# Low halves of 28 mixing-stage weight blocks made by VectorE in two steps

## The chip, the cores and the metric

The kernel runs on one core of a Trainium2 chip. The metric is the device time of one execution in microseconds (us); lower is better. The engines in the text are TensorE (PE, with its weight loads as PEld), VectorE (DVE), ScalarE (ACT), GpSimd (POOL) and SyncE (SP), which here only issues DMAs.

## The reference, cut to what matters

The program is a trunk of two layers over 512 tokens of width 1024, in float32:

```
for l in range(DEPTH):                      # DEPTH = 2
    proj = rms_norm(h, attn_norm[l]) @ w_in[l]
    y_a = rwkv7_mixer(proj[..., :896], ...)          # delta-rule recurrence, 4 heads of 64
    y_b = retention_mixer(proj[..., 896:1920], ...)  # 4 heads of 64
    y_c = mla_mixer(proj[..., 1920:], ...)           # latent attention, 8 heads
    h = h + concat(y_a, y_b, y_c) @ w_out[l]
    h = h + swiglu(rms_norm(h, ffn_norm[l]))         # d_ff = 2816
return rms_norm(h, final_norm)
```

Every weight matrix is read once. The sections on the change deal with how a block of weights is prepared for the matrix unit.

## The kernel before

**Numbers in two halves.** PE multiplies in a rounded 32-bit format (F32R). To keep float32 accuracy each operand is split into a high half, the rounded value, and a low half, what the rounding left over. A product is then three matmuls: high weights with high and with low activations, low weights with high activations (`gemm`, whose matmuls are recorded in `mm`, line 253). The product is kept in PSUM tiles, `pd` for these products and `pm` for everything else, four buffers each.

**The stream of weights.** Weights come as 204 blocks, numbered in the order of use, 102 for each layer; most are 128 partitions by 1024 columns (512 KB). `fetch` (line 397) issues a block's DMA on SP's queue into a raw tile `wr` (three buffers; some blocks of the feed-forward part use the single tile `gg`). `convert` then makes `wh`, the high half, with a cast on ACT (line 419), and `wl`, the low half, with a subtraction `wr - wh` (line 420), each in three buffers. The subtraction is done by DVE, except for the blocks listed in `POOL_LO`, where POOL does it, and those in `DMA_LO`, where a DMA with addition does it (lines 415 to 417) and the loop goes on to the next part before line 420. `wnext` keeps about three blocks converted ahead of the matmul that takes them. Blocks 0 to 33 and 102 to 135 are those of the mixing stages: projections, the up-projections of the latents, and the output projection.

**The order of work.** One generator, `dense`, issues the large products; others (`rwkv`, `chain`, `group_norm`, `retnet`, `head`, `attend`) issue the mixers' small work. A driver interleaves them at recording time by a clock and by the delays of table `T`. PE's instructions keep the recorded order; a scheduler places those of the other engines by its own estimates, so a change in one instruction can move its neighbours.

**Names that are used below.**
- `chain` runs the recurrence over 8 chunks for two pairs of heads, b = 0 and 1. Each step makes `R` (DVE, line 864) from PSUM, which PE multiplies; then PE adds into the state sum and DVE makes the next state `Sb` (line 875), which PE multiplies at the next step.
- Lines 806 and 807 are a serial triangular solve on DVE, 31 dependent pairs, up to 149 us in layer 0.
- Lines 1271 to 1274 (DVE) multiply rotary queries by tables; lines 1275 and 1276 (POOL) add and subtract the products into r tiles, which SP writes out to `ro_d` (line 1278) and reads back as rows of the queries (line 1282). Line 1288 (DVE) scales the other query rows out of PSUM.
- Lines 348 to 351 are an inverse square root: two steps on ACT, two on DVE (350, 351). L959 and L960 square a PSUM tile on ACT, L317 makes its low half, L965 and L966 follow.
- L897 and L899 are the end of a group norm (DVE, then POOL with the gate `gg`); L307 and L308 split the result in halves, which the output projection takes. L1319 adds a product to the residual. L992, L994 and L995 are a softmax's maximum, exponential and reciprocal, and L221 scales by it (on DVE or POOL).

Of the kernel before, what the change touches and what calls it, by code (L numbers as in the profile page):

```python
# [11 lines left out]
F32 = mybir.dt.float32  # L12
# [4 lines left out]
ALU = mybir.AluOpType  # L17
# [21 lines left out]
     {'norm1': 0, 'p_rwkv': 3.01, 'p_ret': 3.04, 'p_head': 0, 'p_gn': 2.97, 'p_att': 4.58, 'p_kr': 6.44, 'rwkv1': 3.33, 'rwkv2': 4.39, 'rwkv3': 0, 'rwkv4': 0.0, 'rwkv5': 0.0, 'rwkv6': 3.29, 'rwkv7': 0.0, 'rwkv8': 8.11, 'rwkv9': 1.7, 'rwkv10': 2.94, 'rwkv11': 0.81, 'rwkv12': 4.08, 'rwkv13': 0.02, 'rwkv14': 0.19, 'rwkv15': 0.58, 'rwkv16': 0, 'rwkv17': 0.73, 'rwkv18': 14.15, 'rwkv19': 0, 'rwkv20': 0.42, 'rwkv21': 0.0, 'chain1': 0.23, 'chain2': 0.96, 'chain3': 0.79, 'group_norm1': 2.86, 'group_norm2': 4.88, 'group_norm3': 11.43, 'retnet1': 1.54, 'retnet2': 4.41, 'retnet3': 0, 'retnet4': 1.97, 'retnet5': 0, 'retnet6': 0, 'head1': 8.22, 'head2': 0, 'head3': 8.59, 'head4': 4.4, 'attend1': 0, 'key_rope1': 1.51, 'latent_norm1': 3.79, 'latent_norm2': 4.98, 'latent_norm3': 0.0, 'sums1': 0.75, 'sums2': 7.46, 'sums3': 2.63, 'sums4': 4.1, 'sums5': 3.51, 'sums6': 8.25, 'sums7': 4.8}]  # L39

EN = {'e499': 'd', 'e535': 'd', 'e541': 'd', 'e542': 'd', 'e563': 'd', 'e564': 'd', 'e565': 'p', 'e592': 'd', 'e593': 'd', 'e594': 'd', 'e595': 'd', 'e757': 'd', 'e759': 'p', 'e773': 'p', 'e826': 'd', 'e968': 'p', 'e969': 'd', 'e970': 'd', 'e909': 'd', 'e1037': 'd', 'e1090': 'd', 'e1096': 'p', 'e1097': 'p', 'e1171': 'd', 'e302': 'd', 'e273': 'd', 'c511': 'a', 'c639': 'a', 'c646': 'a', 'c647': 'a', 'c686': 'a', 'c716': 'a', 'c736': 'a', 'c1008': 'a', 'c498': 'd', 'h1': 'p', 'h2': 'd', 'h3': 'p', 'h4': 'd', 'h5': 'd', 'h6': 'd', 's1': 'd', 's2': 'd', 's3': 'd', 's4': 'd', 'z': 'd', 'x0': 'a', 'x1': 'd', 'x2': 'p', 'x3': 'd'}
NU, NR, NW = 29, 8, 3

AHEAD, FETCH = 3, 2
# [148 lines left out]
def tile_trunk(ctx: ExitStack, tc: tile.TileContext, a: dict, out: bass.AP, dbg=None):  # L193
    nc = tc.nc
    act, dve, pool, sp = nc.scalar, nc.vector, nc.gpsimd, nc.sync
# [17 lines left out]
    def E(key):  # L213
        return {"d": Dve, "p": pool, "a": Act}[EN[key]]

    def times(key, o, x, f):

        if EN[key] == "a":
            act.activation(o, x, AF.Identity, scale=f)
        else:  # L220
            {"d": dve, "p": pool}[EN[key]].tensor_scalar(o, x, f, None, ALU.mult)  # L221

    def nm(s):
        uid[0] += 1
        return f"{s}_{uid[0]}"
# [176 lines left out]
    def raw(at=0):  # L402
        while len(stream["raw"]) <= at:
            fetch()
        return stream["raw"].pop(at)

    def convert(at=0):

        t, src, i, j, parts, on = raw(at)
        hi, lo = (wp.tile([P, i * j], F32R, tag=n, name=nm(n)) for n in ("wh", "wl"))  # L410
        for part in range(parts):
            z = slice(part * i * j // parts, (part + 1) * i * j // parts)
            if on in DMA_LO:

                act.activation(lo[:, z], t[:, z], AF.Identity, scale=-1.0)
                pool.dma_start(lo[:, z], src[:, z], accum_op=ALU.add)
                act.copy(hi[:, z], t[:, z])
                continue
            act.copy(hi[:, z], t[:, z])  # L419
            (pool if on in POOL_LO else dve).tensor_tensor(lo[:, z], t[:, z], hi[:, z].bitcast(F32), ALU.subtract)  # L420
        stream["ready"].append((1.0, tuple(z.rearrange("p (i j) -> p i j", i=i) for z in (hi, lo))))

    def load_next(parts=1):
        plan.pop(0)
        fetch(parts)
        convert()
# [14 lines left out]
    def sums(last, down, end, start):  # L441
# [22 lines left out]
        if not start:  # L464
            s4 = add("s4", s2, a12)
            yield operand(s4)
        else:
            yield convert()
# [3 lines left out]
        if down and not start:  # L472
            yield convert()
# [1041 lines left out]
```

## Time and profile before

| | |
|---|---|
| time, median of 3 runs | 1293.65 us (1290.88 to 1296.6) |
| the profiled execution | 1294.58 us, span 1292.8 us |
| mean granted PE clock | 0.993 |
| PE busy | 1264.5 us (98%) |
| DVE busy | 975.8 us (75%) |
| ACT busy | 697.9 us (54%) |
| POOL busy | 107.4 us (8%) |
| line 420 on DVE, blocks from `wr` | 76 instructions, 87.8 us |
| line 420 on POOL | 15 instructions, 32.8 us |

The span runs from the first to the last instruction of one profiled execution; the 1.78 us beside it lie outside all instructions. [...] Blocks 20 to 33 are prepared between about 131 and 291 us, blocks 116 to 129 between about 730 and 845 us.

### The profile page before, as it was taken

What the parts mean: (1) busy time and instruction counts of PE and PEld (TensorE: products, weight loads), DVE (VectorE), ACT (ScalarE), POOL (GpSimd) and SP (SyncE); (2) the same over time, 40 slices, a digit from 0 to 9 for tenths busy, and PEclk for the clock granted to TensorE, in tenths of its full rate; (3) what the DMA queues carried; (4) which work ended last, traced back from release to release, by engine and by line L of the source; (5) the groups of instructions that cost most, each with busy time, mean ns of one, the idle gap of its engine ahead of it and who ended that gap; (6) DMA issues with size and microseconds to landing.
All of it is one profiled execution on the core that took longest, in us unless ns stands there. A gap on an engine that the chain in (4) does not pass through costs nothing.

```text
span 1292.8 us, 20207 instructions
## 1 busy us (share of the span) xinstructions
PE 1264.5 (98%) x7802; PEld 1087.7 (84%) x7802; DVE 975.8 (75%) x1639; ACT 697.9 (54%) x1302; POOL 107.4 (8%) x93
## 2 busy tenths in 40 slices
PE   7999999999999999999999999999999999999997
PEld 5788778678899999999877877876789999999996
DVE  7786995757987777778747696788579877777774
ACT  7834456835554444445566455485555544444454
POOL 1150011111000000000022310121000000000000
PEclk9999999999999999999999999999999999999998
DMA  7435331033233333332532784241122332223231
GB/s 253 137 90 158 97 108 57 26 98 98 82 115 99 98 98 99 108 105 94 180 110 72 173 170 106 72 159 50 50 98 82 113 100 99 98 99 99 83 113 66
DMA packets 69096, 136.12 MB, mean 105 GB/s; under 512 B 29220, under 2 KB 34116, under 8 KB 69000
## 3 DMA queue, kind: packets, MB, share of 16 engines
q1 hardware_dynamic: 66040, 128.23, 32.0%
q0 software_dynamic: 1728, 5.51, 2.2%
q8 instruction: 61, 1.00, 0.3%
q10 hardware_dynamic: 1232, 1.09, 0.2%
q14 instruction: 35, 0.29, 0.1%
HBM read 122.48 MB, written 9.18 MB: 102 GB/s over the span
## 4 chain that ended last, share of the span: by engine, by line
PE 87%; DVE 7%; ACT 3%; DMA 2%; issue 1%; POOL 0%; SPq 0%; DVEq 0%; ACTq 0%; POOLq 0%
PE pd L253 60%; PE pm L253 25%; PE pm L260 2%; DMA wr<-in_wts_dram 1%; DMA u<-in_xT_dram 1%; DVE wl L420 1%; DVE u L1288 1%; DVE r L806 0%; DVE r L350 0%; DVE r L317 0%; DVE r L1477 0%; DVE u L308 0%; DVE u L1255 0%; DMA PC<-in_prm_dram 0%; DVE r L807 0%
## 5 line engine op out<-in xcount | busy, mean ns | idle before, releaser
L253 PE MATMUL pd<-u,wh 128*128 128x256 f32 (+1 forms) x3136 | 759.9, 335 | 9.5 <-ACT wh L419 6.2
L253 PEld LDWEIGHTS pd<-u,wh 128*128 128x128 f32 x3136 | 530.4, 191 | 72.7 <-issue 7.4
L253 PE MATMUL pd<-u,wl 128*128 128x256 f32 (+1 forms) x1568 | 519.3, 331 | 1.2 <-DVE wl L438 1.0
L253 PEld LDWEIGHTS pd<-u,wl 128*128 128x128 f32 x1568 | 299.4, 191 | 30.3 <-DVE wl L438 1.5
L253 PE MATMUL pm<-u,wh 128*128 128x512 f32 (+1 forms) x800 | 211.8, 352 | 0.0
L253 PEld LDWEIGHTS pm<-u,wh 128*128 128x128 f32 x800 | 139.0, 190 | 17.9
L419 ACT CAST wh<-wr 128x1024 fp32r<-128x1024 f32 (+3 forms) x91 | 88.6, 979 | 116.3 <-issue 58.3
L437 ACT CAST wh<-r 128x512 fp32r<-128x512 f32 x144 | 87.4, 618 | 102.4 <-PE pm L253 51.4
L253 PE MATMUL pm<-u,wl 128*128 128x512 f32 (+1 forms) x400 | 140.3, 351 | 0.0
L420 DVE TENSOR_TENSOR wl<-wr,wh 128x1024 fp32r<-128x1024 f32 (+3 forms) x76 | 87.8, 1158 | 31.1 <-ACT wh L419 30.9
L437 ACT CAST wh<-wr 128x512 fp32r<-128x512 f32 x108 | 67.0, 620 | 79.3 <-PE pm L253 53.8
L438 DVE TENSOR_TENSOR wl<-r,wh 128x512 fp32r<-128x512 f32 x144 | 97.5, 687 | 8.0 <-ACT wh L437 6.0
L438 DVE TENSOR_TENSOR wl<-wr,wh 128x512 fp32r<-128x512 f32 x108 | 74.2, 689 | 24.4 <-ACT wh L437 22.3
L253 PEld LDWEIGHTS pm<-u,wl 128*128 128x128 f32 x400 | 75.7, 189 | 10.3
L1400 DVE TENSOR_TENSOR u<-u,pm 128x512 f32<-128x512 f32 x64 | 43.7, 684 | 43.3 <-PE pm L253 43.3
L420 POOL TENSOR_TENSOR wl<-wr,wh 128x1024 fp32r<-128x1024 f32 (+3 forms) x15 | 32.8, 2193 | 510.6 <-ACT wh L419 510.6
L253 PE MATMUL pm<-u,u 32*32 32x32 f32 (+4 forms) x728 | 66.9, 277 | 0.7 <-DVE u L758 0.2
L253 PEld LDWEIGHTS pm<-u,u 32*32 32x32 f32 (+3 forms) x728 | 50.3, 156 | 18.4 <-issue 10.5
L419 ACT CAST wh<-gg 128x1024 fp32r<-128x1024 f32 x32 | 33.6, 1050 | 42.3 <-issue 27.7
L448 DVE TENSOR_TENSOR r<-r,wr 128x512 f32<-128x512 f32 x72 | 49.5, 687 | 0.6
L420 DVE TENSOR_TENSOR wl<-gg,wh 128x1024 fp32r<-128x1024 f32 x32 | 39.1, 1222 | 7.8 <-ACT wh L419 7.8
L253 PE MATMUL pd<-u,u 96*128 96x512 f32 (+3 forms) x128 | 41.8, 442 | 0.9 <-ACT u L994 0.9
(276 smaller groups left out, 1611.5 us busy)
## 6 DMA issues: line engine op xcount, KB each, us to landing
wr<-in_wts_dram SPq DMA_DIRECT2D x142, 512.0 KB, 3.5
gg<-in_wts_dram SPq DMA_DIRECT2D x32, 512.0 KB, 3.4
wr<-in_wts_dram SPq DMA_DIRECT2D x22, 384.0 KB, 3.0
u<-in_xT_dram SPq DMA_DIRECT2D x7, 512.0 KB, 5.2
wl<-in_wts_dram POOLq DMA_DIRECT2D x5, 512.0 KB, 7.8
tb<-tab_d SPq DMA_DIRECT2D x8, 256.0 KB, 4.5
r<-r SPq DMA_DIRECT2D x32, 64.0 KB, 2.0
h_d<-u SPq DMA_DIRECT2D x4, 512.0 KB, 2.9
```

The lines of the kernel that those rows point to most:

```text
L253: tc.keep_in_program_order(nc.tensor.matmul(o, lhsT, rhs, start=start, stop=stop, skip_group_check=True))
L260: tc.keep_in_program_order(nc.tensor.transpose(o, x, idn))
L419: act.copy(hi[:, z], t[:, z])
L420: (pool if on in POOL_LO else dve).tensor_tensor(lo[:, z], t[:, z], hi[:, z].bitcast(F32), ALU.subtract)
L437: act.copy(hi[:, z], t)
L438: dve.tensor_tensor(lo[:, z], t, hi[:, z].bitcast(F32), ALU.subtract)
L448: E(key).tensor_tensor(o, x, y, ALU.add)
L1288: dve.tensor_tensor(q_[0:64, par, :], ps[rows], fq[rows], ALU.mult)
L1400: dve.tensor_tensor(hk(m), hk(m), ps, ALU.add)
```

## The change

For the 28 blocks of a new tuple `HALVES`, the low half is made by DVE in two subtractions of half the columns each (512 and 512; 384 and 384 for blocks of 768), whatever `POOL_LO` says. The new lines stand behind the branch for `DMA_LO`, which is as before.

```diff
+HALVES = (20, 21, 22, 23, 24, 25, 26, 27, 28, 29, 30, 31, 32, 33, 116, 117, 118, 119, 120, 121, 122, 123, 124, 125, 126, 127, 128, 129)
 ...
             if on in DMA_LO:
 ...
                 continue
             act.copy(hi[:, z], t[:, z])
+            if on in HALVES:
+                for z in (slice(0, i * j // 2), slice(i * j // 2, i * j)):
+                    dve.tensor_tensor(lo[:, z], t[:, z], hi[:, z].bitcast(F32), ALU.subtract)
+                continue
             (pool if on in POOL_LO else dve).tensor_tensor(lo[:, z], t[:, z], hi[:, z].bitcast(F32), ALU.subtract)
```

With `DMA_LO = (113, 114, 115, 118, 119, 120, 121, 122, 124, 125, 126)` and blocks 25, 30, 120, 122 and 127 of the 28 in `POOL_LO`. In the changed kernel the lines from 41 on have moved down by 2 and those behind the new branch by 6; the new subtraction is line 424, and L1288 of before is L1294. PE's order is the same in both kernels. What moves on the other engines:

On DVE in layer 0, from the last two rotary products (L1273, L1274) on. `wl_1836` is block 26. Before:

```order
L1273 TENSOR_TENSOR r_328_1740<-pd_1657,tb_1733 128x512
L1274 TENSOR_TENSOR r_327_1739<-pd_1657,tb_1732 128x512
L1288 TENSOR_TENSOR u_1750<-pd_1759,fB_1592 64x512 x2
L875 SCALAR_TENSOR_TENSOR Sb_317_1721<-pm_1723,dsc_598,EX 128x128
L875 SCALAR_TENSOR_TENSOR Sb_321_1727<-pm_1729,dsc_598,EX 128x128
L420 TENSOR_TENSOR wl_1836<-wr_1833,wh_1835 128x1024
L350 SCALAR_TENSOR_TENSOR r_340_1791<-r_340_1791,r_338_1788 128x512
L864 TENSOR_TENSOR R_342_1814<-pm_1815,EX 128x128
```

The same place in the changed kernel, where `wl_1761` is block 25 and L881, L870, L352 and L353 are L875, L864, L350 and L351 of before:

```order
L1279 TENSOR_TENSOR r_328_1745<-pd_1662,tb_1738 128x512
L1280 TENSOR_TENSOR r_327_1744<-pd_1662,tb_1737 128x512
L424 TENSOR_TENSOR wl_1761<-wr_1758,wh_1760 128x512 x2
L1294 TENSOR_TENSOR u_1755<-pd_1765,fB_1596 64x512 x2
L352 SCALAR_TENSOR_TENSOR r_340_1797<-r_340_1797,r_338_1794 128x512
L881 SCALAR_TENSOR_TENSOR Sb_317_1726<-pm_1728,dsc_598,EX 128x128
L353 SCALAR_TENSOR_TENSOR r_339_1796<-r_340_1797,r_339_1796 128x512
L881 SCALAR_TENSOR_TENSOR Sb_321_1732<-pm_1734,dsc_598,EX 128x128
L972 TENSOR_TENSOR r_338_1794<-pm_1707,r_339_1796 128x512
L870 TENSOR_TENSOR R_342_1820<-pm_1821,EX 128x128
```

Block 25's two halves, which POOL made in one step before, stand ahead of L1288 and Sb; L350 has moved ahead of the first Sb; block 26 has moved behind both R.

On DVE in layer 1, at the same lines. Before:

```order
L1273 TENSOR_TENSOR r_1536_8283<-pd_8237,tb_8276 128x512
L1274 TENSOR_TENSOR r_1535_8282<-pd_8237,tb_8275 128x512
L875 SCALAR_TENSOR_TENSOR Sb_1474_7970<-pm_8255,dsc_7013,EX 128x128
L875 SCALAR_TENSOR_TENSOR Sb_1478_7976<-pm_8262,dsc_7013,EX 128x128
L864 TENSOR_TENSOR R_1543_8319<-pm_8320,EX 128x128
```

In the changed kernel, with block 127 as `wl_8316`:

```order
L1279 TENSOR_TENSOR r_1536_8300<-pd_8254,tb_8293 128x512
L1280 TENSOR_TENSOR r_1535_8299<-pd_8254,tb_8292 128x512
L424 TENSOR_TENSOR wl_8316<-wr_8313,wh_8315 128x512 x2
L881 SCALAR_TENSOR_TENSOR Sb_1474_7987<-pm_8272,dsc_7027,EX 128x128
L881 SCALAR_TENSOR_TENSOR Sb_1478_7993<-pm_8279,dsc_7027,EX 128x128
L870 TENSOR_TENSOR R_1543_8337<-pm_8338,EX 128x128
```

Two halves now stand between the rotary products and the two Sb. On POOL at this place, where block 127 stood between the two rotary sums. Before:

```order
L416 DMA wl_8195<-in_wts_dram 128x768
L1275 TENSOR_TENSOR r_1534_8281<-r_1534_8281,r_1536_8283 128x512
L420 TENSOR_TENSOR wl_8299<-wr_8296,wh_8298 128x1024
L1276 TENSOR_TENSOR r_1535_8282<-r_1535_8282,r_1537_8284 128x512
L221 TENSOR_SCALAR u_8442<-u_8442,rs_8459 128x384
```

In the changed kernel:

```order
L418 DMA wl_8212<-in_wts_dram 128x768
L1281 TENSOR_TENSOR r_1534_8298<-r_1534_8298,r_1536_8300 128x512
L1282 TENSOR_TENSOR r_1535_8299<-r_1535_8299,r_1537_8301 128x512
L223 TENSOR_SCALAR u_8462<-u_8462,rs_8479 128x384
L223 TENSOR_SCALAR u_8498<-u_8498,rs_8515 128x384
```

The second rotary sum follows the first at once. A third place is block 29 in layer 0 on DVE. Before:

```order
L221 TENSOR_SCALAR u_2562<-u_2562,rs_2569 128x512
L420 TENSOR_TENSOR wl_2595<-wr_2592,wh_2594 128x1024
L897 TENSOR_TENSOR r_544_2542<-r_544_2542,u_524 128x512
L995 RECIPROCAL rs_2611<-ssum_2610 128x2
L1319 TENSOR_TENSOR u_2369<-u_2369,pd_2644 128x512
L221 TENSOR_SCALAR r_550_2563<-r_550_2563,rs_2611 128x256
```

In the changed kernel:

```order
L223 TENSOR_SCALAR u_2571<-u_2571,rs_2578 128x512
L424 TENSOR_TENSOR wl_2604<-wr_2601,wh_2603 128x512
L903 TENSOR_TENSOR r_544_2551<-r_544_2551,u_524 128x512
L424 TENSOR_TENSOR wl_2604<-wr_2601,wh_2603 128x512
L1001 RECIPROCAL rs_2621<-ssum_2620 128x2
L1325 TENSOR_TENSOR u_2377<-u_2377,pd_2654 128x512
```

L897 (now L903) goes between the two halves.

## The prediction

> **What bounds the kernel now.** I read the page first, then the busy time of the two stretches in which the changed blocks are made, then the instructions of TensorE (PE) there that had to wait, then what VectorE (DVE) and GpSimd (POOL) did ahead of those waits. From the page, the engines and the two groups of the operation that the change touches:
>
> ```profile
> PE 1264.5 (98%) x7802; PEld 1087.7 (84%) x7802; DVE 975.8 (75%) x1639; ACT 697.9 (54%) x1302; POOL 107.4 (8%) x93
> L420 DVE TENSOR_TENSOR wl<-wr,wh 128x1024 fp32r<-128x1024 f32 (+3 forms) x76 | 87.8, 1158 | 31.1 <-ACT wh L419 30.9
> L420 POOL TENSOR_TENSOR wl<-wr,wh 128x1024 fp32r<-128x1024 f32 (+3 forms) x15 | 32.8, 2193 | 510.6 <-ACT wh L419 510.6
> ```
>
> PE is busy for 98% of the span. A change that touches only DVE and POOL matters where PE waits for them. The changed blocks lie in about 125 to 275 us (layer 0) and 750 to 920 us (layer 1); a row is start and length, then busy time of PE, its weight loads, DVE, ACT and POOL, the granted clock and the DMAs:
>
> ```profile
> 125.00:275.00 150.00, 145.64 (x958) 113.07 (x957) 116.96 (x256) 90.24 (x210) 20.11 (x14) 1.00 0.28 79
> 750.00:920.00 170.00, 164.76 (x1039) 128.47 (x1038) 121.04 (x267) 96.67 (x218) 24.93 (x20) 0.99 0.37 98
> ```
>
> PE's idle time is 4.36 us in the first and 5.24 us in the second. All of it together is 9.6 us, 0.74% of the span: no gain can be larger. The clock is full, so nothing is to be had there. In layer 0 these PE instructions waited where a changed block is near (start, duration, instruction, idle time before it and what ended it):
>
> ```profile
> 172.39 0.49 PE L253 MATMUL pm<-R,u 128*128 128x128 f32 x2 [0.85 <-DVE R L864]
> 177.66 0.49 PE L253 MATMUL pm<-Sb,u 128*128 128x128 f32 x2 [0.44 <-DVE Sb L875]
> 178.76 0.49 PE L253 MATMUL pm<-u,u 128*128 128x128 f32 x2 [0.16 <-ACT u L877]
> 185.67 0.49 PE L253 MATMUL pm<-Sb,u 128*128 128x128 f32 x2 [0.46 <-DVE Sb L875]
> ```
>
> All four belong to the recurrence over chunks: R and Sb are small DVE operations, and what counts is what stands in front of them on DVE. No matmul of these stretches waits for a low half (wl), so a first half that is ready earlier buys nothing.
>
> **What is really changed.** Of the 28 blocks, 118 to 122 and 124 to 126 are in DMA_LO and leave the loop before the new lines: 20 blocks change. 17 of them go from one DVE step to two. Three (25, 30, 127) go from one POOL step to two DVE steps.
>
> **Splitting (17 blocks).** On DVE the next instruction starts before the last one's end, so starts are what to count:
>
> ```profile
> 131.34 1.22 DVE L420 TENSOR_TENSOR wl<-wr,wh 128x1024 fp32r<-128x1024 f32 x1
> 132.47 0.38 DVE L807 TENSOR_TENSOR r<-r,r 128x224 f32<-128x224 f32 x1
> 163.06 0.68 DVE L967 TENSOR_TENSOR r<-r,u 128x512 f32<-128x512 f32 x1
> 163.66 0.68 DVE L1231 TENSOR_TENSOR r<-r,rB 128x512 f32<-128x512 f32 x1
> ```
>
> 1024 columns hold DVE for 1.13 us, 512 for 0.60. Two halves cost 1.20, that is 0.07 more; 17 blocks make 1.2 us. DVE has 33 and 49 us of idle time in the two stretches, which hides it; it counts only where a block stands directly ahead of something PE waits for (one place, below). In the serial triangle solve up to 149 us the extra pieces also fill slots between dependent steps, so I take nothing there. SyncE's queue changes in three places: the ro_d writes go ahead of a weight load twice, and a weight load goes behind the gg load. Those weight loads run up to three blocks ahead of their use, and the products of the blocks in between cover them: nothing. Without that cover such a load would cost its wait for gg.
>
> **Block 25 (layer 0).** Rows of DVE, ACT and POOL around it:
>
> ```profile
> 167.88 2.13 DVE L350 SCALAR_TENSOR_TENSOR r<-r,r 128x512 f32<-128x512 f32 x1
> 172.05 0.28 DVE L864 TENSOR_TENSOR R<-pm,EX 128x128 f32<-128x128 f32 x1
> 175.84 1.38 DVE L1288 TENSOR_TENSOR u<-pd,fB 64x512 f32<-64x512 f32 x2
> 177.26 0.61 DVE L875 SCALAR_TENSOR_TENSOR Sb<-pm,dsc,EX 128x128 f32<-128x128 f32 x2
> 179.03 0.69 DVE L350 SCALAR_TENSOR_TENSOR r<-r,r 128x512 f32<-128x512 f32 x1
> 169.68 0.59 ACT L960 ACTIVATE r<-pm 128x512 fp32r<-128x512 f32 x1
> 167.05 2.41 POOL L420 TENSOR_TENSOR wl<-wr,wh 128x1024 fp32r<-128x1024 f32 x1 [69.69 <-ACT wh L419]
> 175.50 1.28 POOL L1275 TENSOR_TENSOR r<-r,r 128x512 f32<-128x512 f32 x1 [6.04 <-PE pm L253]
> 176.75 1.27 POOL L1276 TENSOR_TENSOR r<-r,r 128x512 f32<-128x512 f32 x1
> ```
>
> The gain: the same L350 takes 0.69 us at 179.03 and 2.13 at 167.88, while POOL makes block 25; it ends at 170.01, 0.55 after POOL. With POOL's step gone, this 1.44 goes. R then starts at about 170.95 instead of 172.05, since the L317 ahead of it (0.60) still needs ACT's L960, which ends at 170.27. That clears PE's 0.85 wait.
>
> The loss: the two halves now stand between L1274 and L1288, and L350 (0.60) moves ahead of Sb. From R to L1288 it was 3.79, so the first half is due at 174.75. L1275, which was at 175.50, comes 1.1 earlier as well: 174.4 to 175.7. The half has two inputs in SBUF as L350 had, so I let it wait and end 0.55 after POOL, at 176.25. Who goes next is told by the only place where two DVE steps met two POOL steps:
>
> ```profile
> 707.13 2.04 DVE L728 TENSOR_TENSOR u<-u,r 64x512 f32<-64x512 f32 x2 [0.57 <-ACT r L719]
> 706.63 1.29 POOL L1162 TENSOR_TENSOR u<-r,tb 128x512 f32<-128x512 f32 x1 [2.83 <-DVE r L1159]
> 707.88 0.66 POOL L733 TENSOR_TENSOR dsc<-r,emid 128x7 f32<-128x7 f32 x1
> ```
>
> They took turns: the second L728 ends at 709.17, 0.63 after L733. So here L1276 (1.27) goes next, and the second half ends near 177.95. Then L1288 twice (1.2) and L350 (0.6): Sb starts at 179.7, 2.45 later than before. PE's rows at 178.76 and 185.67 had 0.16 and 0.46 of waiting, which this lateness eats. Net +1.8 us. Bounds: with no collision the halves end at 175.95, L350 is held by its ACT input until about 177.5 (an estimate: the row at 179.03 less the wait gained), Sb starts at 178.1, net +0.2; with one POOL step waited for, Sb at 178.65, net +0.8.
>
> **Block 127 (layer 1).** The halves again stand right behind L1274, directly ahead of Sb:
>
> ```profile
> 828.52 0.68 DVE L1274 TENSOR_TENSOR r<-pd,tb 128x512 f32<-128x512 f32 x1
> 829.34 0.80 DVE L875 SCALAR_TENSOR_TENSOR Sb<-pm,dsc,EX 128x128 f32<-128x128 f32 x2
> 828.75 1.27 POOL L1275 TENSOR_TENSOR r<-r,r 128x512 f32<-128x512 f32 x1 [8.60 <-DVE r L1273]
> 830.00 2.35 POOL L420 TENSOR_TENSOR wl<-wr,wh 128x1024 fp32r<-128x1024 f32 x1
> 830.43 0.39 PE L253 MATMUL pm<-Sb,u 128*128 128x128 f32 x2
> 843.40 1.22 DVE L420 TENSOR_TENSOR wl<-wr,wh 128x1024 fp32r<-128x1024 f32 x1
> 846.21 1.12 PE L253 MATMUL pd<-u,u 96*128 96x512 f32 x2 [0.86 <-ACT u L994]
> ```
>
> POOL's 2.35 goes, and L1276 moves up behind L1275, onto the halves. The first is due at 829.12, waits for L1275 until 830.02 and ends at 830.57; L1276 runs to 831.8; the second ends at 832.35. Sb starts at 832.3 instead of 829.34, 2.9 late. PE took it 0.40 after its start at 177.66, so at 830.43 there was 0.7 of slack. Net +2.2; +0.3 with no collision, +1.1 with one POOL step. PE has no wait between there and 846.21, so this lateness arrives whole. At 843.40 block 129 holds up the score row maximum behind PE's 0.86 wait: its split adds 0.07, call it 0.1.
>
> **Blocks 29 and 30 (layer 0).** Block 30's halves stand among the residual additions, where POOL is done; cover is DVE's idle time between them. Block 29's halves let L897 in between:
>
> ```profile
> 256.06 1.53 DVE L420 TENSOR_TENSOR wl<-wr,wh 128x1024 fp32r<-128x1024 f32 x1
> 257.51 0.68 DVE L897 TENSOR_TENSOR r<-r,u 128x512 f32<-128x512 f32 x1
> 258.32 1.29 POOL L899 TENSOR_TENSOR r<-r,gg 128x512 f32<-128x512 f32 x1 [1.15 <-PE pd L253]
> 261.04 0.19 PEld L253 LDWEIGHTS pd<-u,wh 128*128 128x128 f32 x1 [0.54 <-DVE u L308]
> ```
>
> L897, POOL's L899, a cast and L308 lead to PE's weight load. L897 can start up to 0.6 earlier, against a wait of 0.54; as block 29 runs stretched beside POOL (1.53 against 1.22) I take -0.4, between 0 and -0.54.
>
> **How sharing is priced.** One pair says that not every POOL operation holds DVE up:
>
> ```profile
> 228.02 0.69 DVE L317 TENSOR_TENSOR r<-u,r 128x512 fp32r<-128x512 f32 x1 [0.68 <-ACT r L314]
> 227.29 1.24 POOL L221 TENSOR_SCALAR u<-u,rs 128x384 f32<-128x384 f32 x1 [5.21 <-DVE rs L995]
> ```
>
> L317 keeps its 0.69 beside a TENSOR_SCALAR; L350 did not beside a TENSOR_TENSOR. L1275 and L1276 are TENSOR_TENSOR, so I price them like L350. [...]
>
> **The sum.** +1.8 + 2.2 + 0.1 - 0.4 = +3.7 us. The profiled execution took 1294.58, of which 1292.8 is the span; it would become 1298.3 with a span of 1296.5. The median of the three runs, 1293.65, is 0.93 below that execution, so the forecast is 1297.3, say 1297.
>
> **Rivals.**
> [...]
> 2. One turn only: both halves run once the first POOL step is over. +0.8 + 1.1 + 0.1 - 0.4 = +1.6: 1295.3.
> 3. Faster, by the relief of DVE at 167.88: if L350's ACT input is early enough for Sb to start before 177.3, the waits 0.85, 0.44, 0.46 and 0.54 all go, 2.3 us, and layer 1 stays: 1291.4. Against it: 1.2 us of halves stand ahead of Sb.
> 4. Clearly slower: R and Sb stay late at each chunk step, so that PE pays for all of DVE's added time: 1.2 for the splits, 3.6 for three blocks, four POOL steps of 1.28, less 1.44: +8.5, 1302. It decides once Sb in both layers starts over 4 us late. Against it: PE's slack between steps.
>
> **Numbers.** Forecast 45%, rival 1 22%, rival 2 18%, rival 3 8%, rival 4 7%. The range takes in rivals 1 and 2 and a bit of what single runs differ by (1290.88 to 1296.6): 1291.5 to 1299.5. A measurement here tells about 0.5%, 6.5 us, from no change. Faster than 1287.2 would need two thirds of all of PE's idle time: 2%. Slower than 1300.1 is rival 4 and the forecast's edge: 8%. Within: 90%.
>
> **What would show it.** In the changed profile L350 in front of the second R should take 0.69; POOL should have 12 of these steps; the first half of block 25 and of block 127 should be stretched to over 1.2 us, with Sb and PE's matmul on it late by 2 us or more. [...] It is wrong altogether if the granted clock moves, or if PE's idle time grows at places with no changed block.

## The result, and the profile after

The changed kernel takes 1298.91 us (median; 1296.67 to 1302.29) where the kernel before takes 1293.74 us: a ratio of 1.0038, with a 95% interval of 1.0025 to 1.0051. That is 5.2 us slower (3.2 to 6.6 by the interval). The profiled execution took 1302.29 us with a span of 1300.5 us; it is the longest of these runs, so its span is read beside two later profiles of the same kernel.

The page of the changed kernel, the engines and the POOL group of the low halves:

```profile
PE 1266.2 (97%) x7802; PEld 1089.7 (84%) x7802; DVE 982.1 (76%) x1662; ACT 697.7 (54%) x1302; POOL 101.6 (8%) x90
L426 POOL TENSOR_TENSOR wl<-wr,wh 128x1024 fp32r<-128x1024 f32 (+3 forms) x12 | 25.7, 2148 | 441.8 <-ACT wh L421 441.8
```

POOL has 12 of these steps instead of 15. DVE is busy 6.3 us longer and PE 1.7 us, while the span is 7.7 us longer: 6.0 us of the added time is PE waiting. Of these, 2.25 us lie before 125 us (idle time 8.08 us before, 10.33 now), where no changed block is made; the two later profiles of the changed kernel have 8.47 and 8.45 us there, so most of the 2.25 belongs to this one execution. The two stretches again, in the columns used ahead of the result:

```profile
125.00:275.00 150.00, 143.27 (x935) 112.96 (x934) 119.84 (x270) 89.64 (x209) 16.17 (x12) 0.98 0.27 76
750.00:920.00 170.00, 163.51 (x1026) 128.50 (x1026) 127.83 (x282) 99.56 (x221) 24.93 (x22) 0.99 0.41 105
```

PE's idle time grew from 4.36 to 6.73 us and from 5.24 to 6.49; in the second stretch the changed kernel runs 5 to 8 us behind, and with the two last waits of the old stretch, which now lie at 926.6 and 927.3, it is 7.40. So 2.4 and 2.2 us were added, 4.5 us in all; the two later profiles give 4.5 and 4.6. The clock of the first stretch, 1.00 before, is 0.98. The PE instructions that carry this:

```profile
180.66 0.80 PE L255 MATMUL pm<-Sb,u 128*128 128x128 f32 x2 [4.27 <-DVE Sb L881]
190.33 0.49 PE L255 MATMUL pm<-Sb,u 128*128 128x128 f32 x2 [0.15 <-DVE Sb L881]
838.13 0.49 PE L255 MATMUL pm<-Sb,u 128*128 128x128 f32 x2 [1.96 <-DVE Sb L881]
854.13 1.13 PE L255 MATMUL pd<-u,u 96*128 96x512 f32 x2 [0.99 <-ACT u L1000]
```

The waits of 0.85 (R), 0.44, 0.16 and 0.46 us in layer 0 are now one of 4.27 and one of 0.15, both at Sb. In layer 1 there was no wait at Sb; now there is one of 1.96. What DVE and POOL did ahead of the first (the second row is the R that PE had waited for, the third the first half of block 25 alone, the fourth both halves):

```profile
167.77 0.69 DVE L352 SCALAR_TENSOR_TENSOR r<-r,r 128x512 f32<-128x512 f32 x1
171.23 0.28 DVE L870 TENSOR_TENSOR R<-pm,EX 128x128 f32<-128x128 f32 x1
175.03 1.49 DVE L424 TENSOR_TENSOR wl<-wr,wh 128x512 fp32r<-128x512 f32 x1
175.03 3.17 DVE L424 TENSOR_TENSOR wl<-wr,wh 128x512 fp32r<-128x512 f32 x2
178.12 1.38 DVE L1294 TENSOR_TENSOR u<-pd,fB 64x512 f32<-64x512 f32 x2
180.25 0.35 DVE L881 SCALAR_TENSOR_TENSOR Sb<-pm,dsc,EX 128x128 f32<-128x128 f32 x1
174.68 1.29 POOL L1281 TENSOR_TENSOR r<-r,r 128x512 f32<-128x512 f32 x1 [76.99 <-PE pm L255]
175.92 1.72 POOL L1282 TENSOR_TENSOR r<-r,r 128x512 f32<-128x512 f32 x1
```

The first half started at 175.03, waited for POOL's first rotary sum (end 175.97) and ended at 176.52, 0.55 us behind it. Then POOL's second sum had its turn (end 177.64), and the second half ended 0.56 us behind that, at 178.20. At the 0.60 us from start to start that 512 columns took in the kernel before (163.06 to 163.66), they would have held DVE for 1.20 us; they held it for 3.09. Layer 1 is the same once more (both halves in one row; the first alone took 1.46 us):

```profile
834.69 3.12 DVE L424 TENSOR_TENSOR wl<-wr,wh 128x512 fp32r<-128x512 f32 x2
837.74 0.60 DVE L881 SCALAR_TENSOR_TENSOR Sb<-pm,dsc,EX 128x128 f32<-128x128 f32 x2
834.33 1.27 POOL L1281 TENSOR_TENSOR r<-r,r 128x512 f32<-128x512 f32 x1 [8.61 <-DVE r L1279]
835.57 1.70 POOL L1282 TENSOR_TENSOR r<-r,r 128x512 f32<-128x512 f32 x1
```

One thing stands in this profile that no term of the sum had, though the forecast had named it as a sign that it is wrong: the granted clock (the third column from the right) falls around the end of the 4.27 us wait and stays low behind it.

```profile
175.00:180.00 5.00, 1.39 (x10) 1.06 (x8) 4.96 (x6) 2.52 (x4) 2.65 (x2) 0.90 0.41 120
180.00:185.00 5.00, 4.34 (x17) 4.15 (x18) 3.85 (x10) 0.82 (x4) 0.00 (x0) 0.50 0.69 194
185.00:190.00 5.00, 5.00 (x26) 4.24 (x25) 3.99 (x7) 1.29 (x4) 0.00 (x0) 0.92 0.04 9
```

Three theories were put to the test. Theory 1: the halves collide with POOL's rotary sums and make Sb late. Theory 2: it is DVE's added work as such (splits, three blocks more) that costs. Theory 3, added later: a long wait of PE also costs clock.

### The profile page after: what moved, and what is told of

It is laid out like the page before. It is cut to its first block, busy times and chain, and to the rows that moved or that the text cites. A ratio compares the mean times of both kernels' runs of the same rounds, so it can differ in the third digit from the quotient of the medians.

```text
span 1300.5 us, 20233 instructions
## 1 busy us (share of the span) xinstructions
PE 1266.2 (97%) x7802; PEld 1089.7 (84%) x7802; DVE 982.1 (76%) x1662; ACT 697.7 (54%) x1302; POOL 101.6 (8%) x90
## 3 DMA queue, kind: packets, MB, share of 16 engines
q10 hardware_dynamic: 1232, 1.09, 0.2%
## 4 chain that ended last, share of the span: by engine, by line
PE 90%; DVE 5%; ACT 3%; DMA 1%; issue 1%; SPq 0%; DVEq 0%; ACTq 0%
PE pd L255 61%; PE pm L255 27%; PE pm L262 2%; DMA wr<-in_wts_dram 1%; DVE wl L424 1%; DVE r L812 0%; DMA u<-in_xT_dram 0%; DVE r L1483 0%; DVE u L1294 0%; DVE r L319 0%; DVE r L813 0%; ACT u L1000 0%; DVE r L744 0%; DVE wl L426 0%; ACT u L309 0%
## 5 line engine op out<-in xcount | busy, mean ns | idle before, releaser
L426 DVE TENSOR_TENSOR wl<-wr,wh 128x1024 fp32r<-128x1024 f32 (+3 forms) x59 | 67.5, 1148 | 27.5 <-ACT wh L421 27.2
L426 POOL TENSOR_TENSOR wl<-wr,wh 128x1024 fp32r<-128x1024 f32 (+3 forms) x12 | 25.7, 2148 | 441.8 <-ACT wh L421 441.8
```

## The experiments

**Which blocks carry the loss.** First the blocks 25 and 127 alone, then the 17 splits alone.

```diff
-HALVES = (20, 21, 22, ..., 33, 116, ..., 129)
+HALVES = (25, 127)
```

> Only blocks 25 and 127 are made in halves by VectorE; the 17 splits and block 30 are as before. In layer 1 the order at the place is that of the changed kernel, in layer 0 only the second half of block 25 stands behind the rotary products, the first stands four microseconds ahead of them. Theory 1 (collision: a half that stands beside the rotary sums waits for GpSimd): layer 1 as in the changed kernel, a wait of PE of 2.0 us at Sb; in layer 0 one half stretched to about 1.4 us instead of two, Sb 1.75 us earlier than in the changed kernel, the wait there about 2.5 us instead of 4.27. Sum against before about +2.8 us, 1296.5. Theory 2 (the 17 splits carry the loss): within 1 us of before.

Measured: 1296.30 us against 1292.48, ratio 1.0031 (1.0019 to 1.0043), by the ratio 4.0 us slower. The half of block 25 that is left behind the rotary products, and PE's two waits at Sb:

```profile
175.09 1.49 DVE L424 TENSOR_TENSOR wl<-wr,wh 128x512 fp32r<-128x512 f32 x1
178.32 0.49 PE L255 MATMUL pm<-Sb,u 128*128 128x128 f32 x2 [1.83 <-DVE Sb L881]
836.69 0.49 PE L255 MATMUL pm<-Sb,u 128*128 128x128 f32 x2 [1.96 <-DVE Sb L881]
```

Layer 1 is as in the changed kernel. In layer 0 the one half took 1.49 us again and the wait was 1.83, less than the 2.5 expected. The waits alone add only 1.9 us to those of before (1.83 and 1.96 in the place of 0.85, 0.44, 0.16 and 0.46); the time is 1.2 us above the expected sum, and in this profile the clock is at 0.68 between 180 and 185 us, which is taken up below.

```diff
-HALVES = (20, 21, 22, ..., 33, 116, ..., 129)
+HALVES = (20, 21, 22, 23, 24, 26, 27, 28, 29, 31, 32, 33, 116, 117, 123, 128, 129)
```

> Only the 17 blocks that VectorE made already are made in halves; 25, 30 and 127 stay with GpSimd in one step. Theory 1 (collision at the rotary sums): no wait of PE over 1 us at either Sb, the time within 1 us of before (0.07 us for each block, 1.2 us, hidden). Theory 2 (the splits carry the loss): 3 to 5 us slower than before.

Measured: 1291.91 us against 1292.48, ratio 0.9999 (0.9988 to 1.0010). The waits in layer 0 are nearly those of before again:

```profile
172.25 0.49 PE L255 MATMUL pm<-R,u 128*128 128x128 f32 x2 [0.85 <-DVE R L870]
177.53 0.49 PE L255 MATMUL pm<-Sb,u 128*128 128x128 f32 x2 [0.43 <-DVE Sb L881]
185.76 0.49 PE L255 MATMUL pm<-Sb,u 128*128 128x128 f32 x2 [0.69 <-DVE Sb L881]
```

So the 17 splits cost nothing that can be measured; theory 2 in this form falls. The loss is in the blocks that moved. The split of block 129 can be seen where it was expected: PE's wait behind it is 0.99 us here and 0.87 in the run with blocks 25 and 127 alone, where block 129 is whole.

**One step instead of two.** Blocks 25 and 127 go to DVE in one step each.

```diff
-HALVES = (20, 21, 22, ..., 33, 116, ..., 129)
+HALVES = ()
-POOL_LO = (0, 8, 12, 13, 25, 30, 35, ..., 122, 127, 130, 137, 140)
+POOL_LO = (0, 8, 12, 13, 30, 35, ..., 122, 130, 137, 140)
```

> Blocks 25 and 127 go to VectorE, but each in one step of 1024 columns; nothing is split, block 30 stays with GpSimd. In the order, block 25 then stands ahead of the rotary products, block 127 right behind them as in the changed kernel. Theory 1 (collision, the two engines taking turns step by step): one step meets one wait. In layer 1 it waits for the first rotary sum alone, ends about 1.1 us after it, and PE's wait at Sb is about 0.9 us instead of 1.96; in layer 0 there is no collision, no wait over 1 us at Sb. Sum against before +0.5 us, 1294.2. Theory 2 (it is VectorE's added work that counts, not the steps): the same lateness in layer 1 as in the changed kernel, 2 us.

Measured: 1294.30 us against 1292.48, ratio 1.0010 (0.9996 to 1.0024). Layer 1:

```profile
832.10 1.99 DVE L426 TENSOR_TENSOR wl<-wr,wh 128x1024 fp32r<-128x1024 f32 x1
834.01 0.60 DVE L881 SCALAR_TENSOR_TENSOR Sb<-pm,dsc,EX 128x128 f32<-128x128 f32 x2
831.73 1.27 POOL L1281 TENSOR_TENSOR r<-r,r 128x512 f32<-128x512 f32 x1 [8.61 <-DVE r L1279]
832.98 2.23 POOL L1282 TENSOR_TENSOR r<-r,r 128x512 f32<-128x512 f32 x1
834.41 0.49 PE L255 MATMUL pm<-Sb,u 128*128 128x128 f32 x2 [0.82 <-DVE Sb L881]
```

The whole block ends at 834.09, 1.09 us behind the first sum, and it is now POOL's second sum that stands still, 2.23 us for work of 1.27. PE's wait is 0.82 us, 0.9 expected. The same columns, cut in two, cost PE 1.96. The number of steps decided here: the one step waited once, the two halves twice.

**The collision taken away.** The changed kernel, with the two rotary sums on DVE.

```diff
-EN = {..., 'e1096': 'p', 'e1097': 'p', ...}
+EN = {..., 'e1096': 'd', 'e1097': 'd', ...}
```

> The changed kernel, with the two rotary sums on VectorE too, so that GpSimd runs nothing beside the halves; VectorE has two more steps ahead of Sb in each layer. Theory 1 (collision): each half takes 0.69 us and holds VectorE for 0.60, the four steps hold it for 2.4 us where the two halves held it for 3.1; Sb is 0.7 us earlier in both layers, PE's waits fall to about 3.6 and 1.3 us, and the time is 1.4 us below the changed kernel's: 1297.5, and lower if the half clock behind the long wait goes too. Theory 2 (no collision, only VectorE's own time ahead of Sb counts): 1.2 us later in each layer, 2.4 us above the changed kernel: 1301.3.

Measured:

```profile
174.69 0.69 DVE L1281 TENSOR_TENSOR r<-r,r 128x512 f32<-128x512 f32 x1
175.89 1.29 DVE L424 TENSOR_TENSOR wl<-wr,wh 128x512 fp32r<-128x512 f32 x2
831.06 1.29 DVE L424 TENSOR_TENSOR wl<-wr,wh 128x512 fp32r<-128x512 f32 x2
179.64 0.49 PE L255 MATMUL pm<-Sb,u 128*128 128x128 f32 x2 [3.56 <-DVE Sb L881]
832.66 0.49 PE L255 MATMUL pm<-Sb,u 128*128 128x128 f32 x2 [1.32 <-DVE Sb L881]
```

Two halves take 1.29 us instead of 3.17, DVE does four steps in less time than it needed for two, and the waits are 3.56 and 1.32 us, 3.6 and 1.3 expected. This shows the collision: DVE has more to do and PE waits less. The time does not follow: 1298.99 us, ratio 1.0050 (1.0035 to 1.0065), where 1297.5 was expected for 0.7 us less waiting in each layer. The mean granted clock of these five runs was 0.990 to 0.994, which leads to theory 3; what is left at equal clock stands at the end of this section.

**Is it the waiting that costs clock?** The changed kernel again, and the changed kernel with TensorE kept busy in the long wait. The extra matmuls write to the tile that the next product clears.

```diff
+            if (l, b, n) == (0, 0, 1):
+                for _ in range(16):
+                    tc.keep_in_program_order(nc.tensor.matmul(ps, blk, EX, start=True, stop=True, skip_group_check=True))
             mm(pR, GL(b, n).rearrange("p w t -> p (w t)"), uv, True, n == 0)
```

> The changed kernel once more, beside before on the same chip, for a second profile. Theory 1 (collision): PE's waits at Sb are 4.3 us in layer 0 and 2.0 us in layer 1 again, 4.5 us more of waiting than in before. Theory 3 (a long wait of PE also costs clock): behind the 4.3 us wait the granted clock is at one half for 3.4 to 6.8 us, as in the first profile, which costs 1.7 to 3.4 us more, in every run; the time 5 to 7 us above before, mean clock lower by 0.001 or more. If the low clock stood there by chance in the first profile, it does not come back at this place.

> The changed kernel with 16 extra matmuls of 512 columns that TensorE runs while it waits for Sb in layer 0; nobody uses their result, and the tile is overwritten by the next product. They fill about 3.7 of the 4.3 us, so Sb comes at the same time as in the changed kernel. Theory 3 (it is the idle TensorE that brings the half clock): no half clock behind 180 us, and the time 1.7 to 2.4 us below the changed kernel run beside it. If the low clock comes from anything else (chance, the load of the chip): a low clock there as often as without the extra matmuls, and no difference in time.

Measured beside the same runs of before (1293.91 us): the changed kernel 1301.31 us, ratio 1.0052 (1.0033 to 1.0072); with the extra matmuls 1297.04 us, ratio 1.0026 (1.0010 to 1.0041), which is more than the 1.7 to 2.4 us of gain expected. First the changed kernel, PE's wait and then the busy times and clock of the 5 us around its end:

```profile
181.54 0.49 PE L255 MATMUL pm<-Sb,u 128*128 128x128 f32 x2 [4.28 <-DVE Sb L881]
```

```profile
180.00:185.00 5.00, 3.46 (x17) 3.27 (x18) 4.47 (x10) 0.83 (x4) 0.00 (x0) 0.74 0.74 213
```

The same two views of the kernel with extra matmuls:

```profile
177.26 3.79 PE L866 MATMUL pm<-EX 128*128 128x512 f32 x16
181.94 0.49 PE L255 MATMUL pm<-Sb,u 128*128 128x128 f32 x2 [0.66 <-DVE Sb L884]
```

```profile
180.00:185.00 5.00, 4.03 (x25) 3.19 (x24) 4.89 (x12) 1.21 (x5) 0.00 (x0) 1.00 0.88 226
```

Sb comes equally late in both (181.13 and 181.53, against 156.10 and 156.48 for the same matmul at the start of the stretch). With PE busy the clock stood at 1.00 there. A second pair, with 7 extra matmuls in front of the late Sb of layer 1 as well:

```diff
+            if (l, b, n) in ((0, 0, 1), (1, 0, 7)):
+                for _ in range(7 if l else 16):
```

> The changed kernel a third time, as the partner of the next run and for one more profile. Theory 1: PE's waits 4.3 and 2.0 us. Theory 3: half clock behind the first wait for 3.4 or 6.8 us once more; 5 to 7 us above before.

> The changed kernel with TensorE kept busy in both waits: 16 extra matmuls in layer 0 as before, and 7 in front of the late Sb of layer 1 (1.6 of its 2.0 us). Theory 3: no low clock behind 180 us nor behind the Sb of layer 1; 2 to 4 us below the changed kernel beside it, and the same lateness of Sb, so that 4 to 5 us above before remain at the same clock. If the low clock comes by chance: no difference from the changed kernel.

Measured beside 1292.87 us for before: the changed kernel 1298.31 us, ratio 1.0048 (1.0032 to 1.0064), a wait of 4.25 us and the clock at 0.66 between 180 and 185 us; both waits filled 1297.74 us, ratio 1.0039 (1.0027 to 1.0052), the clock at 1.00 in both places. Expected were 2 to 4 us below the changed kernel; this pair gives 0.6 us, which alone cannot be told from nothing. All 23 runs of the changed kernel have a mean of 1299.4 us, all 17 with filled waits 1297.4: 2.0 us less, plus or minus 1.3 (twice the standard error). The mean clock was 0.993 and 0.995.

Set side by side, PE's longest wait near 178 to 182 us and the clock behind it:

| kernel | wait, us | lowest clock of a 5 us window, 175 to 190 us |
|---|---|---|
| changed, three profiles | 4.27, 4.28, 4.25 | 0.50, 0.74, 0.66 |
| sums on DVE | 3.56 | 0.66 |
| blocks 25 and 127 alone | 1.83 | 0.68 |
| block 25 by DMA, three profiles (below) | 1.02, 1.02, 1.02 | 1.00, 1.00, 1.00 |
| both kernels with the wait filled | 0.66, 0.62 | 1.00, 1.00 |
| before, splits, whole steps | 0.44, 0.43, 0.34 | 1.00, 1.00, 1.00 |

**The gain alone.** The kernel before with block 25's low half made by an adding DMA, and then the 12 splits of layer 0 with it.

```diff
-DMA_LO = (113, 114, ...)
+DMA_LO = (25, 113, 114, ...)
```

> The kernel before with one change: the low half of block 25 is made by an adding DMA, as it is for blocks 118 to 122, so that neither GpSimd nor VectorE makes it; nothing is split. Theory 1 (collision): L350 in front of the second R takes 0.69 us instead of 2.13, PE's wait of 0.85 us at R goes and the waits of 0.44, 0.16 and 0.46 behind it shrink; 0.9 to 1.9 us faster than before, 1291.2, if nothing else moves. Theory 2 (VectorE's total work sets the end): 1 us at most, no change at these waits.

> As the last one, and with 12 blocks of layer 0 (20 to 24, 26 to 29, 31 to 33) made by VectorE in halves. Theory 1: the splits are hidden, within 0.7 us of the last one. Theory 2: each split costs, 0.8 us or more slower than the last one.

> The kernel before with block 25's low half by an adding DMA, once more, since the first comparison ended at the edge of what can be told (0.999, 0.998 to 1.000). Theory 1: Sb 0.7 us earlier as in the first profile, 0.7 to 1 us faster than before. If that was chance: ratio 1.000.

Measured: ratio 0.9990 (0.9979 to 1.0000) the first time and 0.9998 (0.9988 to 1.0009) the second; with the splits 0.9990 (0.9975 to 1.0004). Rows of the first:

```profile
168.44 0.68 DVE L352 SCALAR_TENSOR_TENSOR r<-r,r 128x512 f32<-128x512 f32 x1
170.97 0.28 DVE L870 TENSOR_TENSOR R<-pm,EX 128x128 f32<-128x128 f32 x1
171.53 0.69 DVE L319 TENSOR_TENSOR r<-r,r 128x512 fp32r<-128x512 f32 x1 [0.27 <-ACT r L966]
177.55 0.49 PE L255 MATMUL pm<-Sb,u 128*128 128x128 f32 x2 [1.02 <-DVE Sb L881]
```

L350's stretch and PE's wait at R are gone, as expected, but the next wait, at Sb, grows from 0.44 to 1.02 us, and the one after it from 0.46 to 0.83, where both were expected to shrink: DVE now idles for ACT (0.27 us) and Sb comes only 0.7 us earlier. PE reaches the Sb matmul of the next step 29.97 us after the one that waited at 155.58, where it took 30.67 before; the second profile has 29.99. A gain of that size lies at the edge of what the plain times tell.

**At equal clock.** Each run on record has its mean granted clock, so the kernels can also be compared at the same clock. This is a reading of the runs above and not one more experiment, and it takes the cost of a lower clock out, also where a wait brings it. A straight line in the clock is fitted, with one offset for each kernel and one for each of the three sets of runs. It goes through 179 runs; two are left out, one of 4411 us and one whose recorded clock of 0.947 does not go with its time of 1293.46 us. The ten runs of the first result are not in it, as the runs of before beside them have no clock on record. The line falls by 0.82 us for each 0.001 of clock, and the offsets are:

| kernel | us above before at equal clock (twice the standard error) | added waiting of PE by the rows, us |
|---|---|---|
| changed, two sets | 4.7 (0.6) | 4.5 |
| waits filled, two sets | 4.5 (0.5) | Sb as late as in the changed kernel |
| sums on DVE | 3.5 (0.9) | 3.1 |
| blocks 25 and 127 alone | 2.3 (0.7) | 1.9 |
| whole steps | 1.2 (0.7) | 0.8 |
| splits | 0.2 (0.7) | 0.5 |
| block 25 by DMA, two sets | -1.0 (0.5) | stretch from 155 us to the second Sb 0.7 shorter |
| block 25 by DMA and 12 splits | -0.9 (0.6) | the same stretch 0.5 shorter |

At equal clock the times follow the waits. Taking the collision away brings 1.3 us, 1.4 expected, though the error is almost as large. Filling the waits brings 0.3 us, so nearly all of the 2.0 us of the plain means is clock. And the two versions with block 25 by DMA come out faster than the kernel before, by 0.07 to 0.08%, which no plain ratio shows clear of its interval.

## Why the prediction was right, point by point

**The direction and the place** were right. 1297.0 was forecast with a range of 1291.5 to 1299.5; 1298.9 came. The number says little by itself: the range also held a kernel with no collision (+0.2 and +0.3 us at the two blocks), rival 2 and a kernel of unchanged time, and of the two later medians of the changed kernel, 1301.31 and 1298.31, one lies outside it. Block 25 was priced too low and the clock was left out, both to the same side, and that the time still fell inside the range is in part luck. What speaks for the mechanism is the rows. The signs that it named for itself are all there: L350 (now L352) at 0.69 us, 12 POOL steps, first halves of 1.49 and 1.46 us, Sb late by over 2 us in both layers.

**Its signs of being wrong.** The forecast was to be "wrong altogether if the granted clock moves, or if PE's idle time grows at places with no changed block". The first came: the clock of the first stretch fell from 1.00 to 0.98, in three of three profiles right at the long wait. The second showed in the first profile alone (the 2.25 us before 125 us). So the collision is what the forecast said, and beside it stands a second cost that it had ruled out.

**Turns, not one wait.** The step that rested on a single place of the trace (707 us) was right: both halves waited, each for one sum. Rival 2 (one wait for both) had Sb some 1.1 us earlier than the forecast in each layer, and so further from what came. A single wait is what the one step of the whole block then showed, 0.82 us of waiting in the place of 1.96.

**Block 25: +1.8 forecast, +2.5 of waiting measured** (4.27 and 0.15 in the place of 0.85, 0.44, 0.16 and 0.46). Sb is 2.75 us late (180.25 against 177.26, less 0.24 by which the whole stretch started later), forecast 2.45. R, at 171.23, is on the old scale at 170.99, forecast 170.95, and PE's wait of 0.85 went as forecast; the first half started at 174.79 on the old scale, forecast 174.75. The halves ended as forecast too (178.20, on the old scale 177.96, forecast 177.95). What was short is the stretch from there to Sb: L1294 and L352 took 2.13 us (178.12 to 180.25), 1.8 were taken. Of the 0.7 us that the term was short, 0.3 is Sb's lateness and 0.15 the wait that is left at the second step, which was counted as eaten; the other 0.2 is that PE had less work time ahead of Sb (from the matmul at 155 us, 25.42 us less the wait of 4.27 is 21.15; before, 22.66 less 0.85 and 0.44 is 21.37).

**Block 127: +2.2 forecast, +2.0 measured.** From the last rotary product (L1274, now L1280) to Sb it is 3.65 us (834.09 to 837.74), 0.82 before: 2.83 late, forecast 2.9.

**Block 129: +0.1 forecast**, 0.99 against 0.86 measured: 0.13.

**Block 29: -0.4 forecast, -0.1 measured.** This step failed: the 0.54 us was idle time of the weight loads, which run ahead (the load before it started at 260.31, its matmul at 260.52), and PE itself had stood still for 0.13 us there. It fell to none; the weight load's idle time to 0.35. By the starts of the matmuls the gain is 0.2 us: the pair at 260.52 took 0.86 us to the next start where others beside it take 0.46, and in the changed kernel the same pair took 0.64. POOL paid for part of it:

```profile
260.79 0.99 DVE L424 TENSOR_TENSOR wl<-wr,wh 128x512 fp32r<-128x512 f32 x1
262.31 0.68 DVE L424 TENSOR_TENSOR wl<-wr,wh 128x512 fp32r<-128x512 f32 x1
260.39 1.51 POOL L223 TENSOR_SCALAR u<-u,rs 128x384 f32<-128x384 f32 x1 [6.02 <-DVE rs L1001]
262.52 1.61 POOL L905 TENSOR_TENSOR r<-r,gg 128x512 f32<-128x512 f32 x1 [0.62 <-issue]
```

Where DVE's half came first it took its 0.68 us, and POOL's step (L899 of before, 1.29) was the one that grew.

**The splits and block 30: nothing forecast.** The splits measured nothing (0.9999). Behind block 30, PE's idle time between 275 and 500 us was 0.58 us before and 0.03, 0.00 and 0.60 in the three profiles of the changed kernel, so nothing is seen there either.

**What the sum lacked** is the clock: a term that it put at nothing. "The clock is full, so nothing is to be had there" was read as if the clock were given; in each of the three profiles of the changed kernel it fell to one half at the wait of 4.25 to 4.28 us. From the matmul that waited at 155 us to the first Sb matmul of the second step it is 35.09, 34.37 and 34.46 us in the three profiles of the changed kernel (155.24 to 190.33 in the first) and 30.67 before. That is 4.4, 3.7 and 3.8 us more, of which 2.5 to 2.6 is waiting: the clock adds 1.9, 1.1 and 1.2. With it the sum is 4.5 of waiting and 1.1 to 1.9 of clock, 5.6 to 6.4 us, against 4.9, 6.7 and 6.2 by the ratios of the three comparisons (1.0038, 1.0052 and 1.0048). The 4.5 us of waiting alone (0.35%) lie in all three intervals too, near the lower end of two; that the clock belongs into the sum rests on the profiles, on the filled waits and on the comparison at equal clock, not on these ratios.

## What to carry to other kernels

Before a step is given to another engine, look at what runs beside it at its new place in the order, not only at what it frees at the old one: here two halves that met two GpSimd steps waited twice (3.09 us in the place of 1.20), and one whole step waited once (1.99 us; 1.22 for such a step at 131.34 in the kernel before). Where the order put the halves directly in front of what the matrix unit waited for, their price was the stretched duration, and the engine's idle time elsewhere, 30 and 42 us in the two stretches, hid none of it. Half clock came with each of the four waits of 3.56 to 4.28 us at Sb and with two of the six of 1.83 to 1.97, so a forecast that makes TensorE stand still that long at one place needs a term for the clock, and a sign of being wrong deserves a price of its own in the sum.

## What the runs showed of the hardware

**Portions of half clock.** The half clock came in fixed portions. In the first profile of the changed kernel 175 to 190 us lack (0.10 + 0.50 + 0.08) x 5 = 3.4 us of full clock, which is 6.8 us at one half; in the other two, and in the kernels with waits of 3.56 and 1.83 us, the same sum gives 1.7, which is 3.4 us at one half. The same holds over the whole run: in all 13 profiles every stretch at one half, except the one at the very end, is 3.41 or 6.83 us long, and the full stretches between two of them are whole multiples of 3.41 us (in the first profile of the changed kernel 491.5, 105.8 and 501.8 us, that is 144, 31 and 147 times 3.413).

**How much idle time brings it.** Carried on from the edges of these stretches, steps of 3.41 us cut each profile into windows. PE's idle time in the windows that hold a wait at Sb, and the clock of the window behind:

| wait, us | idle time in its window, us | clock of the next window |
|---|---|---|
| changed, first profile, layer 0: 4.27 | 2.57, then 1.70 | 0.50, then 0.50 |
| changed, second profile, layer 0: 4.28 | 1.70, then 2.58 | 1.00, then 0.50 |
| changed, third profile, layer 0: 4.25 | 0.98, then 3.27 | 1.00, then 0.50 |
| sums on DVE, layer 0: 3.56 | 2.85 | 0.50 |
| 16 extra matmuls, layer 1: 1.95 | 1.95 | 0.50 |
| blocks 25 and 127 alone, layer 0: 1.83 | 1.83 | 0.50 |
| layer 1 of four profiles: 1.96 or 1.97 | 1.57, 1.55, 1.46, 1.55 | 1.00 |
| block 25 by DMA, layer 0: 1.02 | 1.02 | 1.00 |

So a wait did not have to fill a window: 1.83 us of 3.41 went ahead of half clock. At these places, starting from full clock, the next window was at one half after 1.83 us of idle time and more, and at full clock after 1.70 us and less. In layer 1 nearly the same wait cost clock in one profile of five: there it lay in one window, with all of its 1.95 us, in the others the edge of a window cut it in two, with 1.46 to 1.57 us in the one. Idle time is not all that counts: near 780 us a window with 1.46 or 1.47 us of it was followed by half clock in 10 of 13 profiles, the one of before included, and near 46 and 671 us windows with none were, in 10 and in 9 of 13. What counts there stays open. Between 175 and 190 us no profile without a wait of 1.83 us or more has any half clock.

**Shared time on DVE and POOL.** Beside a TENSOR_SCALAR of GpSimd (L223, 260.39 to 261.90), the first half of block 29 took 0.99 us instead of 0.68; beside a TENSOR_TENSOR (L1281) the first halves of blocks 25 and 127 took 1.49 and 1.46 us and ended 0.55 us after it had ended. What makes the difference between the two stays open.
